# Transposes first, a first projection step of one channel block, and bursts of the modulation tied to chunks

## The chip, the cores and the metric

One core of a Trainium2 chip runs the whole kernel as one program. The metric is the device time of one execution in microseconds (us), from start to end, median of several runs. Engines are called PE (TensorE matmul), PEld (its weight loads), DVE (VectorE), ACT (ScalarE), POOL (GpSimd) and SP (SyncE, which here only issues transfers).

## The reference, cut to what matters

One decoder layer for 256 prompt tokens and 32 sample tokens (8 sequences of 4), 288 tokens in all, model width 2048. The part at issue is the beginning of the layer:

```python
mod = jax.nn.silu(c) @ w_ada + b_ada            # w_ada 2048 x 12288
sh1, sc1, gt1, sh2, sc2, gt2 = jnp.split(mod, 6, axis=-1)
u = ada_modulate(rms_norm(x, norm1_g), sh1, sc1)  # h * (1 + scale) + shift
proj = u @ w_in                                  # w_in 2048 x 9232, split into q k v z a b xpool ga gb
```

Then come a convolution, a gated delta rule, causal pooling, two projections merged by gates, `w_out`, and a feed-forward part; the change touches none of that.

## The kernel before, in words

All activations are kept with channels on the partitions and the 288 tokens along the free axis. The 2048 channels are 16 blocks of 128. A projection is computed in three matmuls for one product: weights and activations are each split into a high part (`wh`, a cast on ACT) and a low part (`wl`, a subtraction on DVE or POOL), and `gemm` adds high times high, high times low and low times high in PSUM. Weights come as chunks of two channel blocks by 512 columns through five `raw` buffers; a chunk gives 24 matmuls of 128x128 by 128x288 into four PSUM banks, which an `evac` function empties.

The modulation is computed by `ada`, a generator. Each of its steps loads rows of `w_ada` and adds their share into one PSUM bank; the last step copies the bank (`adasb`), transposes it and adds the bias into `mod`. The six 2048-wide parts need 16 loads of rows each. Because the projection of a channel block needs `mod` of that block alone, the kernel begins with few blocks: `STEPS` lists the blocks per stage, (0,2), (2,4), (4,8), (8,12), (12,16). In each stage nine panels of 512 columns (`FIRST`) are multiplied with the blocks of the stage and added to nine accumulators `acc` in SBUF. Beside the matmuls of one stage, `fill` runs the generator of the next stage's modulation: after each chunk `fill()` adds `every` to a counter and takes a step for each whole unit.

Ahead of the first stage the inputs are loaded: the three tiles `xt` of x, the constants with the identity `ident` (`cfix`), the conditioning vectors `cs8` and `cp1`, and the small vectors `ra` and `rb`. x is normed (square on ACT, a power on POOL, scaling on DVE), and `normed(q)` transposes four channel blocks on PE through PSUM tiles `px` that ACT copies into `xn`. Before the change only `normed(0)` stands ahead of the first stage and the other three stand in its loop body. In each stage DVE makes `gsc`, applies scale and shift to `xn`, ACT rounds the result to the high part `rq` and DVE takes the low part. `pab` is a narrow matmul on the modulated `xn`, and `pst` transposes of a convolution state.

The order on each engine is not the program's order: a scheduler sets it when the kernel is built, from the data dependencies and its own estimate of durations; an instruction under `tc.high_priority()` goes ahead of others that are ready. `in_turn` keeps the modulation's matmuls in their own order. At run time every engine works off its list strictly in order and waits at an instruction until its operands are there. Transfers are issued by SP in such a list too.

Of the kernel before, what the change touches and what calls it, by code (L numbers as in the profile page):

```python
# [9 lines left out]
F32 = mybir.dt.float32  # L10
# [5 lines left out]
P = 128  # L16
# [8 lines left out]
KB = 2  # L25
# [48 lines left out]
def tile_step(ctx: ExitStack, tc: tile.TileContext, at, t):  # L74
# [29 lines left out]
    def load_raw(srcs, pool=None, kbs=KB):  # L104
        n = KB * 512
        if pool is None:
            raw = wpool.tile([P, n], F32, tag="raw", name="raw", bufs=RAW)
        elif pool is qp:
            raw = fquad("raw").rearrange("p k n -> p (k n)")[:, 0:n]
# [7 lines left out]
    def load_split(srcs, eng=vec):  # L117

        raw = load_raw(srcs)
        wh = [wpool.tile([P, 512], F32R, tag="wh", name="wh", bufs=WH) for _ in range(KB)]  # L120
        wl = [wpool.tile([P, 512], F32R, tag="wl", name="wl", bufs=WH) for _ in range(KB)]
        for i in range(KB):
            act.copy(wh[i], raw[:, i, :])  # L123
            eng.tensor_tensor(wl[i], raw[:, i, :], wh[i].bitcast(F32), ALU.subtract)  # L124
        return wh, wl

    def gemm(srcs_of, xs, evac, kbs, eng=vec, late=False):


        ps = [psg.tile([P, 512], F32, tag="g", name=f"g{j}") for j in range(4)]  # L130
        kbs = list(kbs)
        for c in range(0, len(kbs), KB):
            wh, wl = load_split(srcs_of(kbs[c]), eng)
            for j in range(4):
                o = ps[j][:, 0:N]
                last = c + KB == len(kbs)
                terms = [(w, x, i) for i in range(KB) for w, x in ((wh, 0), (wh, 1), (wl, 0))]
                if late and c == 0:
                    terms.sort(key=lambda v: v[1])
                for n, (w, x, i) in enumerate(terms):  # L140
                    pe.matmul(o, w[i][:, j * P:(j + 1) * P], xs(kbs[c + i])[x], start=c + n == 0,  # L141
                              stop=last and n == 3 * KB - 1)
# [5 lines left out]
    def cols_of(w, c0):  # L148
        return lambda kb: [(w[kb * P:(kb + KB) * P, c0:c0 + 512], 0, 512)]
# [30 lines left out]
    def ada(*d0s, n=16, pool=None):  # L180

        m = n * len(d0s)
        w = m // 4 * P
# [3 lines left out]
        pair = 2 if m == 8 else 1  # L187
        for c in range(0, 16, step * pair):
            loads = []
            for k in range(c, c + step * pair, step):  # L190
                raws = []
                for x in range(per):
                    if per > 1:
                        d = (d0s if len(d0s) > 1 else (d0s[0], d0s[0] + 8))[x]
                        srcs = [(t["w_ada"][0, k * P:(k + 1) * P, d * P:(d + 8) * P], 0, 1024)]
                    else:
                        srcs = [(t["w_ada"][0, k * P:(k + step) * P, d0 * P:(d0 + n) * P], i * n * P, (i + 1) * n * P)
                                for i, d0 in enumerate(d0s)]
                    raws.append(load_raw(srcs, qp if pool and d0s[0] == M_SH1 and k >= 8 else pool, step))
                loads.append((k, raws))  # L200

            todo = [(k, raws, i, j) for k, raws in reversed(loads) for i in range(step) for j in (2, 3, 0, 1)]
            for y, (k, raws, i, j) in enumerate(todo):
                x, q = divmod(j, 4 // per)
# [7 lines left out]
        for i in range(0, w, P):  # L212
            pe.transpose(ps[:, i:i + P], sb[:, i:i + P], ident)
        pv = ps[:, 0:w].rearrange("p (b q m) -> p q b m", q=4, m=32)
        k = 4 // len(d0s)
# [14 lines left out]
    class Fill:  # L230

        gen, every, n = iter(()), 1.0, 0.0

        def __call__(self):
# [11 lines left out]
    STEPS = ((0, 2), (2, 4), (4, 8), (8, 12), (12, 16))  # L246
# [59 lines left out]
    with tc.tile_pool(name="st", bufs=1) as st:  # L306
        cs8 = st.tile([P, P], F32, name="cs8")
        cp1 = st.tile([16, P], F32, name="cp1")
        xt = []
        for i, (src, n) in enumerate(((t["x_prompt"][0, 0:P], P), (t["x_prompt"][0, P:2 * P], P),  # L310
                                      (t["x_sample"].rearrange("b s d -> (b s) d"), NS))):
            xi = st.tile([n, DM], F32, name=f"xt{i}")
            dma(out=xi, in_=src)
            xt.append(xi)
            if i == 0:
                dma(out=cfix, in_=t["consts"][:, c0:c1])
                dma(out=cs8, in_=t["c_sample"].rearrange("b (k c) -> (b k) c", c=P))
                dma(out=cp1, in_=t["c_prompt"].rearrange("b (k c) -> (b k) c", c=P))
# [9 lines left out]
        begin = first_ada(*STEPS[0], st)  # L328
        for _ in range(2):
            next(begin)  # L330
        ra = st.tile([P, P], F32, name="ra")
        rb = st.tile([105, P], F32, name="rb")
        dma(out=ra[0:96, :], in_=t["b_ada"][0].rearrange("(r c) -> r c", c=P))
        dma(out=ra[96:112, :], in_=t["norm1_g"][0].rearrange("(r c) -> r c", c=P))
        dma(out=ra[112:128, :], in_=t["norm2_g"][0].rearrange("(r c) -> r c", c=P))
        dma(out=rb[0:96, :], in_=t["conv_w"][0].rearrange("j (r c) -> (j r) c", c=P))
        dma(out=rb[96:104, :], in_=t["pool_scale"][0].rearrange("(r c) -> r c", c=P))
        dma(out=rb[104:105, :], in_=t["o_norm_g"])
# [7 lines left out]
        drain(begin)  # L346
# [24 lines left out]
        normed(0)  # L371
# [3 lines left out]
        for n, (k0, k1) in enumerate(STEPS):  # L375
# [751 lines left out]
```

## Time and profile before

| what | value |
|---|---|
| median of 3 runs | 1842.74 us (1838.03 to 1844.19) |
| the profiled execution's own time | 1836.14 us |
| its span | 1834.4 us |
| PE busy | 1785.7 us (97%) |
| DVE, ACT, POOL busy | 986.2, 746.4, 206.7 us |
| granted TensorE clock, mean | 0.991 of full speed |
| bytes moved | 371.23 MB, mean 202 GB/s |

The profile is one execution; times in its rows count from the start of the span. Busy time of PE is no measure of work done, since a matmul's end is modelled; the distance between repeated groups in the chain of waits is the better measure. The granted clock stands as a share of 2.4 GHz.

### The profile page before, as it was taken

How to read it: one execution, taken by the hardware profiler on the slowest of the kernel's cores; microseconds unless marked ns; L12 is line 12 of the kernel's file. 1: busy time of each engine (PE TensorE's matmuls, PEld its weight loads, DVE VectorE, ACT ScalarE, POOL GpSimd, SP SyncE). 2: the span in 40 equal slices, each digit the busy share in tenths (PEclk: the TensorE clock that was granted, in tenths of full speed). 3: DMA queues.
4: the chain of work that ended last, by engine and by line, in shares of the span. 5: the costliest groups of instructions: out<-in, count | busy, mean ns of one | idle time of the engine just before them, and what ended most of it. 6: DMA issues, size and time to landing. Idle time of an engine off the chain costs nothing.

```text
span 1834.4 us, 37797 instructions
## 1 busy us (share of the span) xinstructions
PE 1785.7 (97%) x14778; PEld 1657.4 (90%) x14778; DVE 986.2 (54%) x2126; ACT 746.4 (41%) x1522; POOL 206.7 (11%) x376
## 2 busy tenths in 40 slices
PE   5999999999999999999998999999999999999997
PEld 4889998878988787889988999999999999999997
DVE  2466579665645665565555444454444454444454
ACT  4533356433444232344443443443333444444333
POOL 1000025340102232211142000000000000000000
PEclk9999999999999999999999999999999999999999
DMA  9898766666676584876566766655555555555552
GB/s 305 289 322 276 227 204 199 211 213 201 213 244 219 170 253 162 264 255 199 175 217 202 218 198 195 213 181 166 165 168 163 170 163 163 164 169 163 161 160 98
DMA packets 227210, 371.23 MB, mean 202 GB/s; under 512 B 18335, under 2 KB 118168, under 8 KB 226608
## 3 DMA queue, kind: packets, MB, share of 16 engines
q1 hardware_dynamic: 223224, 357.02, 61.0%
q0 software_dynamic: 3808, 11.80, 2.1%
q8 instruction: 116, 1.90, 0.4%
q14 instruction: 62, 0.51, 0.1%
HBM read 361.16 MB, written 7.96 MB: 201 GB/s over the span
## 4 chain that ended last, share of the span: by engine, by line
PE 86%; DMA 6%; DVE 5%; ACT 1%; issue 1%; SPq 0%; POOL 0%; POOLq 0%; ACTq 0%; DVEq 0%
PE g L141 76%; PE ada L206 4%; DMA raw<-in_w_in_dram 3%; DMA raw<-in_w_ada_dram 2%; DVE cy L274 1%; DVE wl L124 1%; PE pss L746 1%; DVE rq L1028 1%; ACT wh L123 1%; PE pks L700 1%; PE py L872 0%; SPq L114 0%; PE py L631 0%; PE pp L636 0%; DMA pw<-in_pool_w_dram 0%
## 5 line engine op out<-in xcount | busy, mean ns | idle before, releaser
L141 PE MATMUL g<-rq,wh 128*128 128x288 f32 x7296 | 1493.2, 299 | 10.3 <-ACT wh L123 4.0
L141 PEld LDWEIGHTS g<-rq,wh 128*128 128x128 f32 x7296 | 1172.9, 188 | 64.4 <-issue 22.7
L141 PE MATMUL g<-rq,wl 128*128 128x288 f32 x3648 | 1075.2, 296 | 0.7 <-POOL wl L124 0.7
L124 DVE TENSOR_TENSOR wl<-raw,wh 128x512 fp32r<-128x512 f32 x910 | 598.8, 692 | 661.4 <-ACT wh L123 659.8
L123 ACT CAST wh<-raw 128x512 fp32r<-128x512 f32 x944 | 543.9, 618 | 878.5 <-PE g L141 630.3
L141 PEld LDWEIGHTS g<-rq,wl 128*128 128x128 f32 x3648 | 687.6, 189 | 7.4 <-issue 4.5
L206 PE MATMUL ada<-raw,cpad 128*32 128x512 f32 (+2 forms) x1152 | 106.6, 473 | 15.3 <-DMA raw<-in_w_ada_dram 14.9
L168 POOL TENSOR_TENSOR ro<-ro,cfix 128x1 f32<-128x1 f32 (+1 forms) x3 | 1.7, 557 | 844.1 <-DVE ro L1091 844.1
L423 DVE TENSOR_TENSOR acc<-acc,g 128x288 f32<-128x288 f32 x144 | 62.2, 449 | 22.7 <-PE g L141 22.4
L206 PEld LDWEIGHTS ada<-raw,cpad 128*32 128x32 f32 x1152 | 28.0, 113 | 39.3 <-issue 19.4
L124 POOL TENSOR_TENSOR wl<-raw,wh 128x512 fp32r<-128x512 f32 x34 | 46.6, 1393 | 45.7 <-ACT wh L123 45.4
L141 PE MATMUL g<-q,wh 128*128 128x288 f32 x256 | 51.0, 294 | 0.0
L274 DVE SCALAR_TENSOR_TENSOR cy<-xc,vb,cy 128x312 f32<-128x312 f32 x72 | 43.6, 623 | 5.3 <-ACT cy L272 4.7
L141 PEld LDWEIGHTS g<-q,wh 128*128 128x128 f32 x256 | 41.3, 189 | 0.0
L141 PE MATMUL g<-q,wl 128*128 128x288 f32 x128 | 37.9, 296 | 0.0
L935 DVE SCALAR_TENSOR_TENSOR x<-g,mod,x 128x256 f32<-128x256 f32 x48 | 23.0, 480 | 12.5 <-PE g L141 11.5
L1061 DVE TENSOR_TENSOR fgg<-fgg,g 128x288 f32<-128x288 f32 x44 | 20.0, 454 | 10.9 <-PE g L141 8.7
L141 PEld LDWEIGHTS g<-q,wl 128*128 128x128 f32 x128 | 24.0, 188 | 0.0
L749 DVE SCALAR_TENSOR_TENSOR sst<-sst,cds,pss 128x128 f32<-128x128 f32 x64 | 18.1, 343 | 7.9 <-PE pss L746 7.7
L1056 DVE SCALAR_TENSOR_TENSOR fgg<-fth,fgg 128x288 f32<-128x288 f32 x44 | 20.0, 455 | 3.9 <-ACT fgg L1055 1.3
L1054 ACT ACTIVATE fth<-g 128x288 f32<-128x288 f32 x44 | 18.1, 412 | 7.3 <-PE g L141 5.4
L644 POOL MEMSET T<- 32x64 f32 x8 | 1.1, 142 | 168.5 <-PE pab L432 151.0
(324 smaller groups left out, 948.4 us busy)
## 6 DMA issues: line engine op xcount, KB each, us to landing
raw<-in_w_gate_up_dram SPq DMA_DIRECT2D x352, 256.0 KB, 3.1
raw<-in_w_in_dram SPq DMA_DIRECT2D x144, 512.0 KB, 5.3
raw<-in_w_ada_dram SPq DMA_DIRECT2D x128, 512.0 KB, 4.4
raw<-in_w_down_dram SPq DMA_DIRECT2D x88, 512.0 KB, 3.8
raw<-in_w_ada_dram SPq DMA_DIRECT2D x128, 256.0 KB, 5.5
raw<-in_w_out_dram SPq DMA_DIRECT2D x32, 512.0 KB, 3.7
raw<-in_w_proj_b_dram SPq DMA_DIRECT2D x16, 512.0 KB, 4.6
raw<-in_w_proj_a_dram SPq DMA_DIRECT2D x16, 512.0 KB, 5.0
```

Source lines behind the costliest of these rows:

```text
L123: act.copy(wh[i], raw[:, i, :])
L124: eng.tensor_tensor(wl[i], raw[:, i, :], wh[i].bitcast(F32), ALU.subtract)
L141: pe.matmul(o, w[i][:, j * P:(j + 1) * P], xs(kbs[c + i])[x], start=c + n == 0, stop=last and n == 3 * KB - 1)
L206: in_turn(pe.matmul(ps[32 * j:32 * j + 32, 0:w], cpad[:, k + i, :], raws[x][:, i, q * w:(q + 1) * w], start=c == 0 and y < 4, stop=c + ste ...
L274: vec.scalar_tensor_tensor(y[:, 0:L], xc[:, m:m + L], vb[:, 24 * m + no:24 * m + no + 1], y[:, 0:L], ALU.mult, ALU.add)
L423: vec.tensor_tensor(a, a, ps, ALU.add)
L700: pe.matmul(pks[NS * i:NS * i + NS, x * P:(x + 1) * P], km[i // 2][:, i % 2, b, :], S[i][:, b, :], start=b == 0, stop=b == NB - 1)
L746: pe.matmul(pss, kt[r, 0, :], wx[b0 // 4][r].rearrange("p b v -> p (b v)"), start=True, stop=True)
L935: vec.scalar_tensor_tensor(x[:, j, 0:NP], ps[:, 0:NP], mod[:, gate + d, 0:1], x[:, j, 0:NP], ALU.mult, ALU.add)
L1028: vec.scalar_tensor_tensor(b[:, d, 0:NP], hp, mod[:, M_SH2 + k, 0:1], a[:, d, 0:NP].bitcast(F32), ALU.add, ALU.subtract)
L1056: vec.scalar_tensor_tensor(gg, th, 1.0, gg, ALU.add, ALU.mult)
L1061: vec.tensor_tensor(gg, gg, ps, ALU.mult)
```

## The change

`STEPS` begins with (0,1), (1,2), (2,4). A chunk of the two one-block stages is one block by 512 columns (`kn`), so it gives 12 matmuls. `ada` learns to make one block of two parts (m = 2): four steps of four row blocks, ended by one matmul with `halves` in place of the transpose. All four `normed(q)` stand ahead of the first stage. The small loads `ra` and `rb` go to POOL's queue and stand early, `cs8`, `cp1` and `cfix` stand before x, and each x tile is loaded in two halves. In the first three stages the steps of the next modulation are tied behind the last matmul of a given chunk (`tc.issue_after`), with a counter set by stage. The first stage's evictions alternate between DVE and ACT, and POOL makes the low parts of three panels in the first stage and of all nine in the second. The copy to `adasb` gets high priority, and the extra buffers of the first modulation are dropped.

```diff
-    STEPS = ((0, 2), (2, 4), (4, 8), (8, 12), (12, 16))
+    STEPS = ((0, 1), (1, 2), (2, 4), (4, 8), (8, 12), (12, 16))
@@ gemm
+        kn = min(KB, len(kbs))
+        for c in range(0, len(kbs), kn):
+            wh, wl = load_split(srcs_of(kbs[c]), eng, kn)
...
-            fill()
+            fill(mm)
@@ ada
-        w = m // 4 * P
+        w = max(m // 4, 1) * P
-        pair = 2 if m == 8 else 1
+        pair = 2 if m in (4, 8) and d0s[0] != M_SH1 else 1
+        step = min(step, 4)
...
-        act.copy(sb[:, 0:w], ps[:, 0:w])
...
+        with tc.high_priority():
+            act.copy(sb[:, 0:w], ps[:, 0:w])
+        if m == 2:
+            pe.matmul(ps[:, 0:64], sb[:, 0:P], halves, start=True, stop=True)
@@ Fill
+        def __call__(self, mm):
             self.n += self.every
             while self.n >= 1:
                 self.n -= 1
-                next(self.gen, None)
+                with tc.issue_after(mm.ins) if self.behind else nullcontext():
+                    next(self.gen, None)
@@ loads
+        dma(out=cs8, in_=t["c_sample"].rearrange("b (k c) -> (b k) c", c=P))
+        dma(out=cp1, in_=t["c_prompt"].rearrange("b (k c) -> (b k) c", c=P))
+        dma(out=cfix, in_=t["consts"][:, c0:c1])
+        dmg(out=ra[0:96, :], in_=t["b_ada"][0].rearrange("(r c) -> r c", c=P))
...
-            dma(out=xi, in_=src)
+            for h in (0, 1024):
+                dma(out=xi[:, h:h + 1024], in_=src[:, h:h + 1024])
@@ stages
-        normed(0)
+        for q in range(4):
+            normed(q)
...
-            if n == 0:
-                for q in range(1, 4):
-                    normed(q)
-            if n == 1:
+            if n == 2:
...
-            fill.every = 8 / (dn // KB * len(FIRST) - 5) if more else 0.4
+            fill.every, fill.n = ((1, -4), (0.5, 0.5), (1, 0), (0.6, 0), (0.6, 0))[n] if more else (0.4, 0)
+            fill.behind = n < 3
...
-                        act.copy(a, ps)
+                        if j % 2:
+                            vec.tensor_copy(a, ps)
+                        else:
+                            act.copy(a, ps)
...
-                gemm(cols_of(w_in, c0), parts(uh, ul), evac, range(k0, k1), gp if n + p == 0 or not more and p % 2 else vec)
+                gemm(cols_of(w_in, c0, min(dn, KB)), parts(uh, ul), evac, range(k0, k1),
+                     gp if (p % 3 == 0 if n == 0 else n == 1 or not more and p % 2) else vec)
```

PE's list of before, from the last transposes that stand between the first chunk and the second. `px` are transposes of x, `ada` steps of the modulation, `g_328` to `g_331` the four banks of the first chunk, `g_393` on those of the second.

```order
L141 MATMUL g_331<-rq,wh 128x288 x2
L141 MATMUL g_331<-rq,wl 128x288
L367 MATMUL px<-cfix,xt_97 128x128 x4
L206 MATMUL ada<-raw,cpad 32x128 x8
L367 MATMUL px<-cfix,xt_92 128x128 x4
L206 MATMUL ada<-raw,cpad 32x128 x8
L432 MATMUL pab<-xn_233,wab 32x288 x2
L367 MATMUL px<-cfix,xt_97 128x128 x4
```

PE's list of the changed kernel from the end of the first modulation (the matmul with `cth`, which holds `halves`) to the first chunk.

```order
L217 MATMUL ada<-cth,adasb 128x64
L376 MATMUL px<-cfix,xt_106 128x128 x4
L376 MATMUL px<-cfix,xt_103 128x128 x4
L444 MATMUL pab<-xn_193,wab 32x288
L376 MATMUL px<-cfix,xt_109 128x32 x4
L376 MATMUL px<-cfix,xt_106 128x128 x4
L376 MATMUL px<-cfix,xt_103 128x128 x4
L376 MATMUL px<-cfix,xt_109 128x32 x4
L376 MATMUL px<-cfix,xt_103 128x128 x4
L376 MATMUL px<-cfix,xt_109 128x32 x4
L140 MATMUL g_287<-rq,wh 128x288
```

The twelve groups of transposes now all stand ahead of the first projection matmul, and `pab` waits among them for the modulated first block.

ACT's list of the changed kernel over the same stretch: copies of transposes (`xn`), the cast of weight chunks (`wh`), the copy of the modulation (`adasb`) and the rounding of the first block (`rq`).

```order
L378 COPY xn_193<-px 128x4x128
L121 CAST wh<-raw 128x512 x2
L378 COPY xn_193<-px 128x4x128
L215 COPY adasb<-ada 128x128
L378 COPY xn_212<-px 128x4x128
L121 CAST wh<-raw 128x512
L378 COPY xn_193<-px 128x4x32
L121 CAST wh<-raw 128x512 x2
L378 COPY xn_212<-px 128x4x128
L378 COPY xn_231<-px 128x4x128
```

Two weight casts stand ahead of the copy of the modulation and three more ahead of the remaining copies of transposes.

PE's list of the changed kernel where the first stage (`g_549` to `g_552` are its last chunk) hands over to the second (`g_581`).

```order
L209 MATMUL ada<-raw,cpad 32x128 x8
L140 MATMUL g_549<-rq,wh 128x288 x2
...
L140 MATMUL g_552<-rq,wh 128x288 x2
L140 MATMUL g_552<-rq,wl 128x288
L217 MATMUL ada<-cth,adasb 128x64
L444 MATMUL pab<-xn_193,wab 32x288
L417 MATMUL pst<-cfix,scv 128x24 x12
L140 MATMUL g_581<-rq,wh 128x288
```

The modulation of the second stage ends behind the last chunk of the first, and nothing but `pab` and `pst` stands between it and the next stage; before, the same end (`L213`) stood four chunks ahead of the first stage's end.

## Rows read from the trace of the kernel before

**Rows 1.** The page: busy tenths of PE in 40 slices of the span.
```profile
PE   5999999999999999999998999999999999999997
```
**Rows 2.** Windows: stretch, length, busy of PE, PEld, DVE, ACT, POOL, clock, DMA share, GB/s.
```profile
20.00:25.00 5.00, 4.65 (x60) 3.02 (x64) 2.07 (x3) 0.59 (x1) 0.54 (x1) 1.00 1.07 362
25.00:30.00 5.00, 3.15 (x58) 2.04 (x59) 0.91 (x4) 2.06 (x5) 1.56 (x2) 1.00 1.07 383
...
35.00:40.00 5.00, 5.00 (x51) 4.47 (x53) 0.39 (x1) 0.80 (x2) 0.00 (x0) 0.73 1.06 381
40.00:45.00 5.00, 3.65 (x37) 2.63 (x30) 2.59 (x4) 4.98 (x13) 0.00 (x0) 0.95 0.93 322
45.00:50.00 5.00, 5.00 (x35) 4.84 (x38) 0.71 (x2) 2.53 (x8) 0.00 (x0) 0.70 1.06 379
```
**Rows 3.** Windows of the second and the third stage of before.
```profile
79.70:118.70 39.00, 39.00 (x356) 33.07 (x356) 28.73 (x64) 12.41 (x23) 0.35 (x2) 1.00 0.91 312
118.70:188.70 70.00, 69.58 (x602) 62.36 (x598) 40.42 (x83) 22.07 (x39) 0.00 (x0) 1.00 0.87 288
```
**Rows 4.** The chain of waits: start, length, what.
```profile
0.75 4.98 DMA xt<-in_x_prompt_dram
6.16 8.04 DMA raw<-in_w_ada_dram
...
84.21 0.85 PE pst L410 x12
...
128.40 6.59 PE g L141 x48
135.00 1.00 PE ada L206 x16
```
**Rows 5.** Timeline from the last modulation step to the first projection matmul.
```profile
25.92 0.65 PE L206 MATMUL ada<-raw,cpad 128*32 128x128 f32 x16 [0.38 <-DMA raw<-in_w_ada_dram]
...
27.75 0.62 ACT L123 CAST wh<-raw 128x512 fp32r<-128x512 f32 x1 [2.15 <-DMA raw<-in_w_in_dram]
28.27 0.26 ACT L211 COPY adasb<-ada 128x128 f32<-128x128 f32 x1
...
29.85 1.56 DVE L388 TENSOR_SCALAR xn<-xn,gsc,mod 128x256 f32<-128x256 f32 x2
...
31.89 0.67 ACT L395 CAST rq<-xn 128x576 fp32r<-128x576 f32 x1 [2.68 <-DVE xn L392]
...
32.62 0.79 PE L141 MATMUL g<-rq,wh 128*128 128x288 f32 x4 [1.50 <-ACT rq L395]
```
**Rows 6.** Groups by line and form, 0 to 240 us: busy us, mean ns.
```profile
L124 DVE TENSOR_TENSOR wl<-raw,wh 128x512 fp32r<-128x512 f32 x100 | 65.0, 687 | 66.5 <-ACT wh L123 66.5
...
L423 DVE TENSOR_TENSOR acc<-acc,g 128x288 f32<-128x288 f32 x97 | 42.3, 451 | 19.6 <-PE g L141 19.4
...
L369 ACT COPY xn<-px 128x512 f32<-128x512 f32 x8 | 4.6, 588 | 14.2 <-PE px L367 14.2
...
L395 ACT CAST rq<-xn 128x1152 fp32r<-128x1152 f32 x3 | 3.5, 1155 | 2.4 <-DVE xn L392 2.4
...
L124 POOL TENSOR_TENSOR wl<-raw,wh 128x512 fp32r<-128x512 f32 x2 | 2.5, 1271 | 7.0 <-ACT wh L123 7.0
```
**Rows 7.** The scaling of xn on DVE, 0 to 240 us: ns min/median/max.
```profile
L388 DVE TENSOR_SCALAR xn<-xn,gsc,mod x16: 401/408/1237, 29.9 to 229.7; 128x256 f32<-128x256 f32 x16
```
**Rows 8.** Timeline at the end of the second stage of before.
```profile
112.51 1.38 DVE L388 TENSOR_SCALAR xn<-xn,gsc,mod 128x256 f32<-128x256 f32 x4
...
118.42 0.69 PE L432 MATMUL pab<-xn,wab 128*32 128x288 f32 x8
```
**Rows 9.** Windows of 20 us with a shorter and a longer wait of PE.
```profile
280.00:300.00 20.00, 18.74 (x142) 16.46 (x139) 19.00 (x36) 13.07 (x34) 12.75 (x25) 1.00 0.68 215
...
380.00:400.00 20.00, 17.86 (x109) 14.70 (x110) 11.50 (x38) 7.30 (x23) 7.69 (x11) 0.83 0.72 222
```
**Rows 10.** Window of the load of the narrow weights (wab).
```profile
33.00:34.00 1.00, 1.00 (x10) 0.80 (x9) 0.36 (x1) 1.00 (x4) 0.00 (x0) 1.00 1.06 141
```

More of the change, by code (lines that the diff above doesn't have):

```diff
@@ L115, in load_raw, with load_split @@
         return raw
[L117 to L124, printed above, removed]
+    def load_split(srcs, eng=vec, kn=KB):
+        raw = load_raw(srcs, kbs=kn)
+        wh = [wpool.tile([P, 512], F32R, tag="wh", name="wh", bufs=WH) for _ in range(kn)]
+        wl = [wpool.tile([P, 512], F32R, tag="wl", name="wl", bufs=WH) for _ in range(kn)]
+        for i in range(kn):
+            act.copy(wh[i], raw[:, i, 0:512])
+            eng.tensor_tensor(wl[i], raw[:, i, 0:512], wh[i].bitcast(F32), ALU.subtract)
         return wh, wl
@@ L131, in gemm @@
         kbs = list(kbs)
-        for c in range(0, len(kbs), KB):
-            wh, wl = load_split(srcs_of(kbs[c]), eng)
+        kn = min(KB, len(kbs))
+        for c in range(0, len(kbs), kn):
+            wh, wl = load_split(srcs_of(kbs[c]), eng, kn)
             for j in range(4):
                 o = ps[j][:, 0:N]
-                last = c + KB == len(kbs)
-                terms = [(w, x, i) for i in range(KB) for w, x in ((wh, 0), (wh, 1), (wl, 0))]
+                last = c + kn == len(kbs)
+                terms = [(w, x, i) for i in range(kn) for w, x in ((wh, 0), (wh, 1), (wl, 0))]
                 if late and c == 0:
@@ L140, in gemm @@
                 for n, (w, x, i) in enumerate(terms):
-                    pe.matmul(o, w[i][:, j * P:(j + 1) * P], xs(kbs[c + i])[x], start=c + n == 0,
-                              stop=last and n == 3 * KB - 1)
+                    mm = pe.matmul(o, w[i][:, j * P:(j + 1) * P], xs(kbs[c + i])[x], start=c + n == 0,
+                                   stop=last and n == 3 * kn - 1)
                 if last:
@@ L198, in ada @@
                                 for i, d0 in enumerate(d0s)]
-                    raws.append(load_raw(srcs, qp if pool and d0s[0] == M_SH1 and k >= 8 else pool, step))
+                    raws.append(load_raw(srcs, pool, step))
                 loads.append((k, raws))
             todo = [(k, raws, i, j) for k, raws in reversed(loads) for i in range(step) for j in (2, 3, 0, 1)]
+            if m == 2:
+                todo = [(k, raws, i, 2 * (i % 2) + h) for k, raws, i, j in todo if j == 0 for h in (1, 0)]
             for y, (k, raws, i, j) in enumerate(todo):
-                x, q = divmod(j, 4 // per)
+                x, q = divmod(j % m, 4 // per)
                 with tc.high_priority() if y else nullcontext():
@@ L210, in ada @@
         sb = wpool.tile([P, 512], F32, tag="adasb", name="adasb", bufs=1)
-        act.copy(sb[:, 0:w], ps[:, 0:w])
[L212 to L215, printed above, removed]
+        with tc.high_priority():
+            act.copy(sb[:, 0:w], ps[:, 0:w])
+        if m == 2:
+            pe.matmul(ps[:, 0:64], sb[:, 0:P], halves, start=True, stop=True)
+            pv = ps[:, 0:64].rearrange("p (b q m) -> p q b m", q=2, m=32)
+            k = 1
+        else:
+            for i in range(0, w, P):
+                pe.transpose(ps[:, i:i + P], sb[:, i:i + P], ident)
+            pv = ps[:, 0:w].rearrange("p (b q m) -> p q b m", q=4, m=32)
+            k = 4 // len(d0s)
         for i, d0 in enumerate(d0s):
@@ L230, in tile_step @@
     class Fill:
-        gen, every, n = iter(()), 1.0, 0.0
-        def __call__(self):
+        gen, every, n, behind = iter(()), 1.0, 0.0, False
+        def __call__(self, mm):
             self.n += self.every
@@ L308, in tile_step @@
         cp1 = st.tile([16, P], F32, name="cp1")
+        dma(out=cs8, in_=t["c_sample"].rearrange("b (k c) -> (b k) c", c=P))
+        dma(out=cp1, in_=t["c_prompt"].rearrange("b (k c) -> (b k) c", c=P))
+        dma(out=cfix, in_=t["consts"][:, c0:c1])
+        ra = st.tile([P, P], F32, name="ra")
+        rb = st.tile([105, P], F32, name="rb")
+        dmg(out=ra[0:96, :], in_=t["b_ada"][0].rearrange("(r c) -> r c", c=P))
+        dmg(out=ra[96:112, :], in_=t["norm1_g"][0].rearrange("(r c) -> r c", c=P))
+        dmg(out=ra[112:128, :], in_=t["norm2_g"][0].rearrange("(r c) -> r c", c=P))
+        dmg(out=rb[0:96, :], in_=t["conv_w"][0].rearrange("j (r c) -> (j r) c", c=P))
+        dmg(out=rb[96:104, :], in_=t["pool_scale"][0].rearrange("(r c) -> r c", c=P))
+        dmg(out=rb[104:105, :], in_=t["o_norm_g"])
         xt = []
@@ L327, in tile_step @@
                                  chf.rearrange("p (m k) -> p m k", k=16), ALU.add, ALU.mult)
[L328 to L338, printed above, removed]
+        halves = cth[:, 0:64]
+        gp.tensor_tensor(halves, ident[:, 0:64], ident[:, 64:P], ALU.add)
         pv = aux("pv")
```

13 lines of the change are left out of this document (4 added, 9 removed).

## Prediction

> **What bounds the kernel now.** I read the page first, then windows, then the chain of waits, then timelines. On the page PE is busy in every slice but the first [rows 1]: whatever this change gains, it gains in the first 190 us, where the stages of the first projection stand. There the chain begins with transfers: x, then the first modulation's weights (8.04 us in one piece) [rows 4]; in the timeline the last step of that modulation runs at 25.92 us, and the first projection matmul follows at 32.62 [rows 5]. From then on PE is full, with two blemishes: ACT is full from 40 to 45 us while PE waits for transposes, and the clock is at 0.73 and 0.70 in two windows, that is at the lower of its two levels for part of them, after PE had idled [rows 2]. The second stage of before takes 39.0 us with PE busy all the time, the third 70.0 us with 0.42 us idle [rows 3]. In these stages a projection matmul costs 6.59/48 = 0.137 us and 16 modulation records 1.00 us [rows 4].
>
> So the change can move three things: when the first projection matmul starts, what is lost inside the first two channel blocks, and what is lost between stages. Later work is the same in kind and count.
>
> **The start.** The first modulation shrinks from two blocks to one: 16 transfers of 256 KB become 8, 4.2 MB become 2.1 MB, but the rows become half as long (512 bytes in place of 1024), 4096 of them as before. No row of before shows rows of 512 bytes in number, so I bound: at the rate by bytes, 362 to 383 GB/s where transfers queue [rows 2], 2.1/0.37 = 5.7 us; if each row costs as much as one of 1024 bytes, 4.2/0.37 = 11.3 us. I take 6.5 us, near the first end, as bytes have set the rate in every busy window. The Trainium skill (DMA: Bandwidth & Descriptors, section "Why small descriptors are slow") speaks against the short rows: each packet carries a fixed overhead of about 3 beats beside one beat for 32 bytes, so 19 beats for 512 bytes against 35 for 1024. By that rule alone, an estimate, the load takes 5.7 x 38/35 = 6.2 us; no row of before shows it.
>
> Step by step: the first transfer of x is issued at 0.75 and 1.05 MB of it has landed at 5.73 [rows 4]; at 0.37 MB per us that is 2.8 us of data behind 2.15 us of latency, so data flows from 2.9 us. x and the small inputs, 2.5 MB, are in at 9.7, the modulation at 16.2, the first two weight chunks (0.52 MB) at 17.6. ACT's list has two weight casts and one copy ahead of the copy `adasb`: 0.62 + 0.59 + 0.26 us [rows 5, 6] make it 19.1, so the modulation ends behind the weights, as it did at 27.75 and 28.27 [rows 5]. The next three chunks wait for `wab`, whose transfer of tiny rows pulled the rate to 141 GB/s at a full DMA share [rows 10]; I price it at 1.5 us, and chunks three to five are cast by 17.6 + 1.5 + 3 x 0.65 + 0.65 = 21.7. Behind them ACT has five copies of 0.59 [rows 6] and two of tiles a quarter as wide, about 0.29 each by their share and a fixed part, about 1.5 us of waits between PE and ACT over two PSUM tiles, and the rounding of one block (half of 0.67, rows 5): 5.4 us. First projection matmul at 27.3, against 32.62. The loads moved off SP's list to POOL's queue end before 12 us and nothing waits for them; POOL is free there.
>
> **First stage, one block.** 9 panels x 12 matmuls = 108 x 0.137 = 14.8 us, and the second modulation, 64 records at 0.65/16 [rows 5], 2.6 us. Six of the twelve groups of transposes stood in this stretch in before; they are gone from it. ACT has per panel one cast and two evictions, DVE a subtraction and two, less than PE's 1.65 us. One spell at the lower level of the clock when the work sets in, as in before: 0.73 and 0.70 over 5 us are 1.35 and 1.5 us lost, with edges in the neighbouring window (0.95) [rows 2]: 1.7 us. End at 46.4.
>
> **Handovers.** The new cost. A stage's modulation now ends in or behind the last chunks of the stage before, so the chain from there to the rounded blocks lies open. First to second: matmul with `halves` 0.2, bias and scale vector 0.8, scaling of one block 0.35 to 0.8, samples 0.45, then `pab` and the 12 `pst` transposes, 0.85 [rows 4], which also need their own late load: 3.1 us, 2.0 of them idle. Second to third: DVE's list has the last evictions, 2 scalings (0.35 each, by 4 in 1.38) [rows 8], samples, a weight subtraction, then the rounding 0.67 [rows 5]: 3.2 us, 2.85 idle. Third to fourth: four scalings 1.38, two subtractions 1.3, the last eviction and small ones 1.5, rounding 1.15 [rows 6, 8], together 5.4 us, of which two bursts and `pab` cover 2.8; idle 2.6, against about 0.6 in before. Queued behind the waiting PE are only projection matmuls, and nobody but DVE and ACT evictions waits for these.
>
> In before the scaling took 0.78 us a block while POOL made low parts, up to 1.24 against a median of 0.41 [rows 5, 7]. POOL now makes 12 in the first two stages, each 1.27 us [rows 6]; I count one collision, in the first handover. The Trainium skill (SBUF — State Buffer, section "Who interferes with whom") says that DVE and GpSimd lock a common port pair for a whole instruction; the trace agrees, 1.24 us against 0.41. By that rule each of the first two handovers could wait one such instruction, 1.3 us more each.
>
> **Second stage, one block.** 14.8 us, its bursts 128 records at 0.65/16 = 5.2, the other `pst` 0.85. DVE has 36 additions of 0.45 and some six subtractions of 0.65 [rows 6], 20.1 us against PE's 20.8, so I add 1.0 for banks that come free late: 21.8 us.
>
> **Third stage** is before's second (blocks 2 and 3, the same bursts): 39.0 less 1.7 of `pst` and 0.3 of `pab`, 37.0 us. **From the fourth on** the stages are before's third to fifth.
>
> **The sum.** 27.3 + 17.4 + 1.7 = 46.4; + 3.1 + 21.8 = 71.3; + 3.2 + 37.0 = 111.5. Before reaches this point at 118.4 [rows 8]. 6.9 us ahead; less 2.0 for the longer third handover, 4.9. Handovers also cost clock: a window with 1.26 us of idle PE kept 1.00, one with 2.14 us shows 0.83 [rows 9]. I count one spell of 1.7 us in expectation (three handovers, about half each is 2.5; the third is broken up by bursts). 3.2 us faster: 1836.14 - 3.2 = 1832.9 against the profiled execution. The median is 6.6 us above that execution, and I carry the difference over: 1842.74 - 3.2 = **1839.5 us**.
>
> **Rivals.** *Clearly faster:* casts do not hold the copies up (first matmul at 24.5, 2.8 earlier), no clock spell in a handover (1.7), DVE keeps up (1.0): 8.7 us, 1834.0. For it: ACT is busy only 0.59 of 20 to 25 us in before [rows 2]. Against: its list puts the casts first, and they wait for transfers.
>
> *Slower:* the bursts tied to chunks wait for their transfers. In the third stage each chunk with its burst needs 1.57 MB in 24 x 0.137 + 1.00 = 4.3 us, 366 GB/s; two bursts are loaded ahead, six are not. Each us lost per period counts six times, so the gain is gone when a period takes 4.3 + 3.2/6 = 4.8 us, at 325 GB/s. At 288, the mean of the next stage in before [rows 3], a period takes 5.45 and the loss is 6 x 1.15 = 6.9, so 3.7 us slower than before: 1846.4; from 273 GB/s down it is slower by more than a measurement's reach. For it: the tie takes away the scheduler's freedom. Against: where transfers queue, windows show 362 to 383 GB/s [rows 2], and before drew the same bytes through the same buffers with PE full [rows 3].
>
> *The short rows cost as long ones:* 4.8 us later start, 1844.3, no change that can be told.
>
> *It does not do what it says:* the lists show that transposes, blocks and bursts stand where the change puts them, so this is small.
>
> **Chances.** Forecast as worked out 0.42, clearly faster 0.28, slower 0.14, short rows 0.12, something else 0.04. About 0.3% (5.5 us) is what a measurement can tell from no change. Faster by more needs below 1837.2: nearly all of the second case and a tenth of the first, 0.32. Slower by more needs above 1848.3: the third case mostly, and what the reordering behind 190 us may bring, 0.16. The same: 0.52. Range 1830 to 1848.5: the low end is all of the clearly faster case and handovers as cheap as before's; the high end takes in the short rows, two more clock spells and a late `pst` load.
>
> **What would show it.** Right: first projection matmul near 27 us, idle gaps of 2 to 3 us at three handovers, near 46, 71 and 112 us, third stage near 37 us, fourth beginning 3 to 5 us earlier than 118.7. Wrong: a start after 31 us; waits of PE for `w_ada` transfers in the third stage; a difference that arises behind 190 us, where I expect none.

## The result, and the profile after

| | kernel before | changed kernel |
|---|---|---|
| median of 10 runs each | 1841.78 us | 1851.75 us |
| lowest to highest | 1834.8 to 1844.19 | 1846.55 to 1857.74 |
| the profiled execution's own time, its span | 1836.14, 1834.4 us | 1854.41, 1852.6 us |
| granted TensorE clock, mean | 0.991 | 0.985 |

The ratio is 1.0065, 95% interval 1.0045 to 1.0085: slower by 0.65%, where I forecast 1839.5 us and gave slower 0.16. The profiled execution of the changed kernel is 2.7 us above its median and that of before 5.6 below its own, so of the 18.3 us between the two profiles 10.0 are in the medians. The page's slices answer to [rows 1]: busy tenths of PE, then the granted clock.

```profile
PE   6899999989999999999999999999999999999997
...
PEclk8999999989999999999999999999999999999998
```

The weaker second slice (46 to 93 us) is new, and so is the one around 390 us, with a lower clock. The windows of the changed kernel answer to [rows 2]:

```profile
20.00:25.00 5.00, 3.68 (x37) 2.36 (x35) 3.52 (x8) 3.50 (x8) 2.24 (x2) 1.00 0.87 254
25.00:30.00 5.00, 3.22 (x18) 2.04 (x18) 1.04 (x2) 3.19 (x7) 0.30 (x1) 0.74 0.88 254
30.00:35.00 5.00, 4.28 (x19) 3.82 (x20) 0.73 (x2) 1.87 (x5) 0.00 (x0) 0.50 0.92 281
35.00:40.00 5.00, 5.00 (x30) 5.00 (x30) 3.36 (x8) 3.44 (x9) 1.44 (x1) 0.73 0.73 224
...
50.00:55.00 5.00, 2.53 (x31) 2.19 (x30) 3.42 (x9) 2.14 (x6) 2.55 (x2) 0.97 0.97 321
55.00:60.00 5.00, 4.59 (x22) 3.58 (x23) 0.71 (x3) 0.84 (x2) 0.35 (x2) 0.50 0.74 232
```

Two things stand out: a first projection that starts at half the clock, 1.2 in place of 2.4 GHz (0.50 from 30 to 35 us; before works so at its start too, for less time [rows 2]), and a hole at 52 us, where PE is busy 2.53 of 5 us and works at half the clock afterwards (0.50). The timeline of the changed kernel shows this first handover, from block 0 to block 1:

```profile
52.20 0.33 PE L217 MATMUL ada<-cth,adasb 128*128 128x64 f32 x2
...
53.00 1.26 POOL L122 TENSOR_TENSOR wl<-raw,wh 128x512 fp32r<-128x512 f32 x1 [1.07 <-ACT wh L121]
53.04 1.25 DVE L387 SCALAR_TENSOR_TENSOR gsc<-mod,va 128x9 f32<-128x9 f32 x1
54.32 0.41 DVE L398 TENSOR_SCALAR xn<-xn,gsc,mod 128x256 f32<-128x256 f32 x1
...
55.11 1.17 PE L444 MATMUL pab<-xn,wab 128*32 128x288 f32 x2 [2.58 <-DVE xn L402]
...
56.58 1.44 PE L417 MATMUL pst<-cfix,scv 24*128 24x24 f32 x12 [0.30 <-DMA scv<-in_state_conv_dram]
57.95 0.74 PEld L140 LDWEIGHTS g<-rq,wh 128*128 128x128 f32 x3
```

The end of the second modulation (the matmul with `halves`, L217) stands behind the last chunk of the first stage. From there PE has nothing to do until DVE has made `gsc` and `xn`: 2.58 us. `gsc`, 0.17 us at 80 us, takes 1.25 beside POOL's subtraction. Then `pab` and `pst` run at half the clock, and the first matmul of block 1 stands at 57.95, 5.6 us after the last of block 0. The waits of PE in the changed kernel from 50 to 130 us (total, times, longest) show this wait at all three handovers: 2.58, 2.67 and 0.31 us. The third handover waits 1.0 us for modulation weights besides.

```profile
PE pab L444 <- DVE xn L402: 5.6, 3, 2.7
PE ada L209 <- DMA raw<-in_w_ada_dram: 1.0, 1, 1.0
```

In time, by the end of the last eviction of each stage:

| end of blocks | before | changed | difference |
|---|---|---|---|
| 0 and 1 | 79.96 | 81.28 | +1.3 |
| 2 and 3 | 118.98 | 123.25 | +4.3 |
| 4 to 7 | 188.96 | 196.19 | +7.2 |
| 8 to 11 | 256.45 | 266.26 | +9.8 |
| 12 to 15 | 329.69 | 342.25 | +12.6 |

Where an expectation below names such an end, it counts 0.24 us less. The remaining 5.7 us of the two profiles lie behind 342 us, where the work is the same; there the changed kernel's execution spends 38.6 us at half the clock, before 27.2.

Where the 12.6 us are can be counted from two windows, before first and the changed kernel second (in the fences, row 1 is 32 to 196 us, row 2 is 196 to 330):

```profile
32.00:196.00 164.00, 161.61 (x1410) 141.72 (x1411) 89.25 (x182) 65.72 (x133) 0.35 (x2) 0.98 0.89 296
196.00:330.00 134.00, 131.62 (x1010) 119.64 (x1010) 99.23 (x220) 70.26 (x156) 37.97 (x74) 1.00 0.65 204
```

```profile
32.00:196.00 164.00, 155.65 (x1401) 136.16 (x1405) 102.65 (x223) 54.17 (x103) 13.38 (x12) 0.96 0.85 284
196.00:330.00 134.00, 129.13 (x998) 116.19 (x991) 94.28 (x212) 65.77 (x150) 36.20 (x74) 0.99 0.67 213
```

Idle time of PE in the first stretch: 2.4 us before, 8.4 after. The clock's share that is missing: 0.02 x 164 = 3.3 before, 0.04 x 164 = 6.6 after. In the second stretch idle time is 2.4 and 4.9, and the clock costs 1.3 more. Sum: 6.0 + 3.3 + 2.5 + 1.3 = 13.1, against 12.6 by the ends of the stages. The two agree partly by chance: up to blocks 4 to 7 the terms give 9.3 against 7.2, since seven of the twelve groups of transposes (28 matmuls) stand behind the first projection matmul in before and ahead of it in the changed kernel, less two bursts that before has ahead of it, an estimate of some 2 us; behind that they give 3.8 against 5.3. So waits and half-clock work make up the loss, to within about 2 us on either side of 196 us.

The clock's share is not all behind handovers. These windows split it, two of the changed kernel and then two of before:

```profile
32.00:52.60 20.60, 20.53 (x178) 18.88 (x178) 10.17 (x22) 12.51 (x31) 7.91 (x6) 0.86 0.81 242
52.60:61.50 8.90, 6.09 (x34) 4.79 (x38) 4.43 (x12) 1.62 (x4) 1.61 (x3) 0.62 0.72 237
```

```profile
32.00:79.70 47.70, 45.73 (x404) 39.66 (x405) 16.16 (x30) 29.25 (x70) 0.00 (x0) 0.93 0.90 298
79.70:83.70 4.00, 4.00 (x39) 3.25 (x39) 2.21 (x6) 1.04 (x3) 0.00 (x0) 1.00 0.72 192
```

In the changed kernel 0.14 x 20.6 = 2.9 us lie in the start of the projection and 0.38 x 8.9 = 3.4 behind the first handover; the other two handovers have 1.00. Before loses 0.07 x 47.7 = 3.3 in its start and nothing in its handover at 80 us, where PE is busy all 4.0 us. Up to 196 us the extra clock is that of the first handover alone.

### The profile page after: what moved, and what is told of

Read it like the earlier page. It is cut to its first block, busy times and chain, and to the rows that moved or that the text cites. A ratio compares the mean times of both kernels' runs of the same rounds, so it can differ in the third digit from the quotient of the medians.

```text
span 1852.6 us, 37896 instructions
## 1 busy us (share of the span) xinstructions
PE 1792.3 (97%) x14781; PEld 1662.6 (90%) x14781; DVE 1004.7 (54%) x2176; ACT 742.1 (40%) x1506; POOL 220.8 (12%) x393
## 3 DMA queue, kind: packets, MB, share of 16 engines
q1 hardware_dynamic: 227494, 356.90, 60.5%
## 4 chain that ended last, share of the span: by engine, by line
PE 91%; DMA 4%; DVE 2%; ACT 1%; issue 1%; SPq 1%; POOL 0%; POOLq 0%; ACTq 0%; DVEq 0%
PE g L140 79%; PE ada L209 5%; DMA raw<-in_w_ada_dram 2%; PE pss L758 1%; DMA raw<-in_w_in_dram 1%; DVE rq L1040 1%; PE pks L712 0%; DMA xt<-in_x_prompt_dram 0%; PE py L884 0%; SPq L112 0%; PE py L643 0%; DMA raw<-in_w_gate_up_dram 0%; DVE hp L1038 0%; PE pp L648 0%; DVE wl L122 0%
## 5 line engine op out<-in xcount | busy, mean ns | idle before, releaser
L434 DVE TENSOR_TENSOR acc<-acc,g 128x288 f32<-128x288 f32 x180 | 77.7, 450 | 31.9 <-PE g L140 31.7
L122 POOL TENSOR_TENSOR wl<-raw,wh 128x512 fp32r<-128x512 f32 x44 | 59.7, 1375 | 61.8 <-ACT wh L121 47.3
L947 DVE SCALAR_TENSOR_TENSOR x<-g,mod,x 128x256 f32<-128x256 f32 x48 | 23.0, 479 | 12.5 <-PE g L140 11.5
```

The lines of the kernel that those rows point to most:

```text
L122: eng.tensor_tensor(wl[i], raw[:, i, 0:512], wh[i].bitcast(F32), ALU.subtract)
L947: vec.scalar_tensor_tensor(x[:, j, 0:NP], ps[:, 0:NP], mod[:, gate + d, 0:1], x[:, j, 0:NP], ALU.mult, ALU.add)
```

## The experiments

My theory after reading the two traces was that the tie of the bursts to chunks lets each modulation end in the last chunk of its stage, so that three handovers lie open and drop the clock (A; the windows above show the drop at the first alone). Rivals: the transposes ahead hold the start up (B); the one-block steps by themselves cost (C); the new loads do (D); it is not the tie, but the counters `fill.n` and `fill.every`, which set the bursts late (E). The ratio is to the kernel before on the same chip. Idle is PE's from 32 to 196 us and the clock that of the same window, as above; the last column is the end of blocks 12 to 15 in us (in before 329.69).

| kernel | ratio, 95% interval | idle | clock | end |
|---|---|---|---|---|
| the change | 1.0065 [1.0045, 1.0085] | 8.4 | 0.96 | 342.25 |
| e2 transposes back in the loop | 1.0064 [1.004, 1.0088] | 11.5 | 0.97 | 341.86 |
| e8 unread matmuls in the handovers | 1.0041 [1.0022, 1.0061] | (2.2) | 0.98 | 337.03 |
| e5 tied, early counters | 1.0038 [1.0021, 1.0054] | 8.1 | 0.99 | 334.54 |
| e9 third stage untied | 1.0018 [1.0001, 1.0034] | 5.0 | 0.98 | 330.82 |
| e10 first two stages untied | 1.0011 [0.9997, 1.0025] | 3.5 | 0.98 | 332.67 |
| e6 untied, counters of the change | 1.0009 [0.9989, 1.003] | 2.1 | 1.00 | 327.93 |
| e7 two blocks first, untied | 1.0008 [0.9988, 1.0028] | 3.4 | 0.98 | 330.94 |
| e3 untied, early counters | 0.9998 [0.998, 1.0016] | 2.2 | 0.98 | 329.22 |
| e1 two blocks first | 0.9985 [0.9973, 0.9998] | 5.0 | 0.98 | 332.85 |
| e11 the same again | 1.0008 [0.9992, 1.0023] | 5.3 | 0.96 | 332.85 |
| e4 the loads alone | 0.9983 [0.9963, 1.0004] | 0.8 | 0.98 | 327.28 |
| e12 the same again | 0.9995 [0.9976, 1.0014] | 2.4 | 0.97 | 331.13 |

The unread matmuls of e8 count as busy, hence the brackets. One profile tells the end to within some 4 us (e4 and e12 are one kernel); in kernels that start with two blocks some of the idle time is a later start. The clock of one window is no sure sign either: e11 has 0.96 as the change has, and no loss.

**e1 and e11: a first stage of two blocks, bursts tied in the first two stages.** With the one-block second stage go its nine low parts on POOL, and the counters are early ones; the rest of the change is kept.

```diff
-    STEPS = ((0, 1), (1, 2), (2, 4), (4, 8), (8, 12), (12, 16))
+    STEPS = ((0, 2), (2, 4), (4, 8), (8, 12), (12, 16))
...
-            fill.every, fill.n = ((1, -4), (0.5, 0.5), (1, 0), (0.6, 0), (0.6, 0))[n] if more else (0.4, 0)
-            fill.behind = n < 3
+            fill.every, fill.n = ((1, 0), (1, 0), (0.6, 0), (0.6, 0))[n] if more else (0.4, 0)
+            fill.behind = n < 2
...
-                     gp if (p % 3 == 0 if n == 0 else n == 1 or not more and p % 2) else vec)
+                     gp if (p % 3 == 0 if n == 0 else not more and p % 2) else vec)
```

> The changed kernel with the old first step of two blocks, all else of the change kept (transposes ahead, new loads, tied bursts in the first two stages). Theory A (open handovers: each stage's modulation ends so late that the chain to the next stage's blocks lies open, 2.6 us of idle PE each, with clock spells): one handover of three is gone, about 4 us faster than the changed kernel, near 1848. Theory B (the transposes ahead of the first matmul cost the gain of the start): no gain, the first projection matmul later than 32.4 us, near 1852. Theory C (the one-block steps as such, with a chunk of 12 matmuls and an eviction per 12): near before, 1842 to 1844.

> The changed kernel with a first stage of two blocks, bursts tied in the first two stages, once more on another day and chip: it was 0.9985 [0.9973, 0.9998]. If it is really faster than the kernel before, the ratio is again below 1 and both intervals together exclude 1; if the first was chance, near 1.000 to 1.002, as the same kernel with free bursts was.

Measured 1839.98 us, and again 1841.5 (both on one chip, though the second expectation says another): the loss is gone, but together they are no gain over before. That is more than A expected (1848) and nearer to C, so the one-block steps are needed for the loss; whether they cost by themselves e3 tells. So the tie, with these counters, costs nothing where the first stage has two blocks; its modulation ends at 60.5 us there, well ahead of the end of the stage at 75.16. Neither the transposes ahead (B) nor the loads (D) cost, as both are in this kernel.

**e2: `normed(1)` to `normed(3)` back in the loop of the first stage.**

```diff
-        for q in range(4):
-            normed(q)
+        normed(0)
...
+            if n == 0:
+                for q in range(1, 4):
+                    normed(q)
```

> The changed kernel with three of the four groups of transposes back in the first stage. Theory B: first projection matmul at about 27 us in place of 32.4, blocks 0 and 1 done 4 to 6 us earlier, near 1847. Theory A: the transposes run later at the full clock, a gain of 2 us at most, and the three handovers are unchanged: near 1850.

Measured 1855.07, ratio 1.0064. B falls. Its timeline shows why the start does not gain; the first two rows are the rounding and the first projection matmul:

```profile
26.04 0.43 ACT L404 CAST rq<-xn 128x288 fp32r<-128x288 f32 x1
...
27.11 1.33 PE L140 MATMUL g<-rq,wh 128*128 128x288 f32 x4
...
31.02 2.82 PE L376 MATMUL px<-cfix,xt 128*128 128x128 f32 x16
...
34.64 0.30 PEld L140 LDWEIGHTS g<-rq,wh 128*128 128x128 f32 x2
```

The first projection matmul stands at 27.11, 5.3 us earlier than in the changed kernel, and then the transposes stand between the chunks: the first panel's eviction ends at 36.13 us, against 36.14. For the start the transposes cost the same in either place.

**e3: untied, and counters that do the modulations early.**

```diff
-            fill.every, fill.n = ((1, -4), (0.5, 0.5), (1, 0), (0.6, 0), (0.6, 0))[n] if more else (0.4, 0)
-            fill.behind = n < 3
+            fill.every, fill.n = ((1, 0), (1, 0), (2, 0), (0.6, 0), (0.6, 0))[n] if more else (0.4, 0)
+            fill.behind = False
```

> The changed kernel with the bursts not tied and due earlier in their stage (one step per chunk in the one-block stages, two per chunk in the third), as the old rate had it. Theory A: idle PE at the handovers goes from 2.6, 2.7 and about 2 us to under 1 each and two clock spells go: 6 to 9 us faster than the changed kernel, 1843 to 1846. Theory B: the start stays at 32 us and the gain is 2 us at most. A rival to A (bursts that come earlier wait for their transfers): idle PE before modulation steps rises by what the handovers give, near 1851.

Measured 1842.28, ratio 0.9998. The loss is gone with one-block steps and transposes ahead in place: C falls as far as it means a cost that must come with the steps. One-block steps and the tie cost together, and neither does alone (e3, e1). The timeline of e3 where the first stage ends has no hole, and adds of the second stage (L434) follow the last copy of the first (L430) at once:

```profile
56.69 0.46 DVE L430 COPY acc<-g 128x288 f32<-128x288 f32 x1 [1.53 <-PE g L140]
...
57.09 2.06 DVE L434 TENSOR_TENSOR acc<-acc,g 128x288 f32<-128x288 f32 x5
```

**e4 and e12: the kernel before with the loads of the change alone** (`cs8`, `cp1`, `cfix` ahead of x, x in halves, `ra` and `rb` on POOL's queue).

> The kernel before with the change's loads alone (small inputs first, x in halves, vectors on the POOL queue). If the loads cost (the POOL queue's packets or the order delay x and the first modulation): 2 to 4 us slower than before, 1844 to 1846. If they help: first projection matmul 2 to 3 us earlier than 32.6, 1839. Theories A and B: no loss from it, 1840 to 1842.

> The kernel before with the changed kernel's loads alone (order of the small loads, x in halves, two loads on POOL's queue), once more: it was 0.9983 [0.9963, 1.0004]. If these loads gain what the end of the first projection showed (327.0 us against 329.45 in the kernel before, 2.4 us), the ratio is 0.9987 again and both runs together lie below 1. If it was chance, 1.000 to 1.001.

Measured 1839.99 and 1841.93: no loss, and no gain that two runs bear out. D falls.

**e5: tied, with e3's counters.** The diff is e3's pair of lines on `fill.every` and `fill.n`, with `fill.behind = n < 3` kept.

> The changed kernel with its bursts still tied behind chunks, but due earlier (one step per chunk in the one-block stages, two in the third). If lateness is the cause: the handovers of the second and third stage close, 5 to 9 us faster than the changed kernel, 1843 to 1847. If the tie itself is the cause (PE waits in order for the burst's transfer): no gain, idle PE ahead of modulation steps of 5 us or more in sum, 1850 or later.

Measured 1846.79, ratio 1.0038: in between. The open handover is nearly gone from the waits of PE, 33 to 132 us, but another wait stands ahead of it:

```profile
PE ada L209 <- DMA raw<-in_w_ada_dram: 3.1, 3, 1.4
PE g L140 <- ACT acc L432: 1.1, 1, 1.1
...
PE pab L444 <- DVE xn L402: 0.3, 1, 0.3
```

Tied to early chunks, the bursts wait for their weights instead. Against e3, where the tie is the only difference, it is 0.40% slower, clear of both intervals: the tie costs without the late counters too. That lateness is a part of the tie's cost rests on less, 0.27% against an uncertainty of about 0.26, and on the handovers' wait (0.3 us against 5.6).

**e6: untied, with the counters of the change.**

```diff
-            fill.behind = n < 3
+            fill.behind = False
```

> The changed kernel with the tie alone taken away, its counters kept; the order of PE then has the modulation's end well before the end of the first two stages. If the tie is the cause: as good as the kernel with free and earlier bursts, 1842 to 1844. If the counters (which set how late a burst is due) are the cause: no gain, 1850 to 1853.

Measured 1842.91, ratio 1.0009, with the tie as the only difference: 0.56 of the 0.65% come back. Its view of L217 says how (ns min/median/max, first and last start); the changed kernel's is the second fence:

```profile
L217 PE MATMUL ada<-cth,adasb x4: 217/274/323, 22.4 to 38.2; 128*128 128x64 f32 x4
```

```profile
L217 PE MATMUL ada<-cth,adasb x4: 218/275/323, 22.0 to 52.3; 128*128 128x64 f32 x4
```

Untied, the second modulation ends at 38.2 us, 15 us ahead of the end of the first stage; tied, at 52.3, behind its last chunk. The counters are the same: without the tie the scheduler puts a burst where its weights are there. So E falls as a cause by itself: late counters without the tie cost nothing that can be told. The window of e6 to 196 us closes the account:

```profile
32.00:196.00 164.00, 161.95 (x1476) 141.97 (x1477) 106.59 (x233) 57.95 (x110) 13.18 (x12) 1.00 0.90 303
```

Idle time is 2.1 against 8.4 us and the clock 1.00 against 0.96: 6.3 + 6.6 = 12.9 us, and blocks 4 to 7 end 12.3 us earlier than in the changed kernel (183.89). Of the 6.6, 2.9 are the changed kernel's start, as the windows above show; in e6's execution the half-clock work of the start lies ahead of 32 us.

**e7: e1 with untied bursts at before's rate** (`fill.every = 8 / (dn // KB * len(FIRST) - 5)`, `fill.behind = False`).

> The old steps (two blocks first) with the new loads, all transposes ahead, and bursts free at the old rate: what is left of the change is its start. If the open handovers are the whole loss, the start's gain shows: blocks 0 and 1 done at about 75 us as in the kernel with two blocks and ties, no open handover behind, 1835 to 1838, faster than before by 4 to 7 us. If the start gives nothing in the end: 1840 to 1842.

Measured 1841.99, ratio 1.0008: with two blocks first the tie makes no difference that can be told (e1 and e11).

**e8: the change, with six matmuls of 128x256 whose results nobody reads, at the end of each of the first three stages:** in the first behind the matmul with `halves` (`fill.tail`), in the others behind the last projection matmul.

```diff
-            pe.matmul(ps[:, 0:64], sb[:, 0:P], halves, start=True, stop=True)
+            fill.tail = pe.matmul(ps[:, 0:64], sb[:, 0:P], halves, start=True, stop=True)
...
+            if n < 3:
+                warm = aux("warm", 2)
+                for _ in range(6):
+                    with tc.issue_after(fill.tail.ins if n == 0 else mm.ins):
+                        pe.matmul(warm[:, 0:256], ident, cpad.rearrange("p k m -> p (k m)")[:, 0:256], start=True, stop=True)
```

> The changed kernel with six matmuls of 128x128 by 128x256 behind the end of each of the first three stages, whose results nobody reads: PE is busy while the chain of the handover runs. If the spells at the lower clock are a part of the loss: the spell that begins at 54.7 us goes, blocks 0 and 1 are done 2 to 3 us earlier than 81.0, about 3 us faster, 1848 to 1850. If the chain alone counts: no change or up to 2 us slower, 1851 to 1854.

Measured 1847.17, ratio 1.0041: 0.24 of the 0.65% come back, which is not clear of the two intervals (some 0.28 together), and the handovers stay as long. The half-clock stretch behind the first one is shorter, 3.4 us (from 55.95) against 6.8 (from 54.74), but not gone, as `pst` there waits 1.4 us for its own load (0.3 in the changed kernel). That this is the work of the unread matmuls is not shown: e9, which has none, has 3.4 us there too (from 55.56). And e8 ends block 0 1.8 us ahead of the changed kernel, though the engines' lists up to there are the same in the two kernels, and block 1 only 0.9 ahead. So e8 does not tell what keeping PE busy is worth; what the clock costs is read from the windows of the changed kernel, 3.4 us behind the first handover.

**e9 and e10: untied in the third stage only, and in the first two only** (`fill.behind = n < 2`, and `n == 2`).

> The bursts are tied to chunks in the first two stages only; in the third they stand where the scheduler puts them. Theory (the two short handovers with their idle 2.6 us and the half-clock stretches behind them carry most of the cost of the tie): only the third stage (34.7 us from its first eviction to its last in the changed kernel, 32.9 without any tie) and the third handover (12.4 us against 10.7) come back, 3.6 us; blocks 4 to 7 end near 192.4 us (195.95 in the changed kernel, 183.65 without any tie), median near 1848.5, ratio 1.004. Rival (the third stage's tied bursts are what costs): the median comes back to 1843, ratio within 1.001.

> The reverse: tied in the third stage only. Theory: the first two handovers close, 9 us earlier at the end of blocks 4 to 7 (near 187 us), median near 1845, ratio 1.002; PE shows no wait over 1.3 us between 30 and 90 us. Rival (third stage): nothing comes back but what the idle time itself was worth, median 1849 to 1851.

Measured 1844.66 (1.0018) and 1841.72 (1.0011). The gains do not add: 0.47 and 0.54%, and 0.56 with both. By the end of blocks 4 to 7, in one execution each, they do: 7.3 and 5.7 us, and 12.3 with both (e6). What does not add lies behind, where no burst is tied. Both times came back further than I expected, e10's though its blocks 4 to 7 end at 190.45, not near 187. Of e9's 7.3 us, 4.4 lie between the end of block 1 and the first evicted panel of blocks 4 to 7, near the 3.6 expected; the rest lies ahead of the stage that was changed, a start 1.0 us earlier and a shorter half-clock stretch at 55 us. Its first handover keeps its wait (2.6). Besides, both kernels have no longer wait than 0.8 and 1.0 us in place of one that the changed kernel has later:

```profile
PE ada L209 <- DMA raw<-in_w_ada_dram: 3.3, 1, 3.3
```

This one of the changed kernel, at 272.85 us, has a half-clock stretch from 276.61 behind it, and the stage of blocks 12 to 15 takes 70.0 us from its first evicted panel, against 65.8 in e9. e6 and e1 have it too, with 2.4 and 2.0 us, so it is not the tie's alone; why the third stage's order moves it was not tried.

## Why the prediction was wrong

**What held.** The handovers are where I put them, two of them with the idle time forecast: 2.58 and 2.67 us, where I wrote 2.0 and 2.85. The second stage took 22.2 us (forecast 21.8), the handover to the third 3.37 (3.2). The rival of tied bursts that wait for transfers in the third stage did not come true there. The chain of waits of the changed kernel has a period of 4.39 us, where I said 4.3, and no wait in it:

```profile
87.25 1.00 PE ada L209 x16
88.25 3.40 PE g L140 x24
91.64 1.00 PE ada L209 x16
92.64 3.39 PE g L140 x24
```

**The step that failed: the start.** "First projection matmul at 27.3" was the whole gain; it stood at 32.40, against 32.62 before. The term behind it is the rate of the first transfers. I took 0.37 MB per us from 2.9 us on, and 6.5 us for the modulation's 2.1 MB; the windows of the changed kernel show less:

```profile
0.00:10.00 10.00, 1.11 (x3) 0.54 (x3) 0.56 (x2) 3.76 (x5) 4.94 (x17) 1.00 0.72 241
10.00:15.00 5.00, 0.32 (x8) 0.35 (x12) 1.48 (x3) 2.86 (x3) 1.10 (x2) 1.00 1.14 269
15.00:18.00 3.00, 2.69 (x37) 1.79 (x29) 2.35 (x3) 1.15 (x2) 0.54 (x1) 1.00 1.11 334
18.00:21.00 3.00, 3.00 (x38) 1.77 (x36) 0.89 (x5) 1.70 (x3) 0.55 (x1) 1.00 0.97 217
```

Up to 10 us they carry 2.41 MB, where I had 2.63: 0.6 us late. From 10 to 18 us, where nearly all of the modulation's short rows run, they carry 5 x 0.269 + 3 x 0.334 = 2.35 MB, so its load took close to 8 us, 1.5 more than my 6.5. From 18 to 21 us, with weight chunks and the short rows of `wab`, the rate is 217 GB/s, which is 1.2 us late again. Only from 15 to 18 us is it 334 GB/s, at which 2.1 MB take 6.3 us. By the Trainium skill (DMA: Bandwidth & Descriptors, "Why small descriptors are slow") it was 6.2, an estimate; this row comes near it, the load as a whole does not.

So the fifth chunk is cast by 25.87, not 21.7 (+4.2, of which these rows show 3.3; what made the other 0.9 is open), as the timeline shows. The copies of the transposes then alternate with PE at half the clock and end the start at 32.4 (+0.9; the terms add to 27.1, and the prediction carries 27.3):

```profile
25.25 0.62 ACT L121 CAST wh<-raw 128x512 fp32r<-128x512 f32 x1 [1.29 <-DMA raw<-in_w_in_dram]
...
31.20 0.58 ACT L378 COPY xn<-px 128x512 f32<-128x512 f32 x1 [1.21 <-PE px L376]
31.68 0.43 ACT L405 CAST rq<-xn 128x288 fp32r<-128x288 f32 x1
...
32.40 1.57 PE L140 MATMUL g<-rq,wh 128*128 128x288 f32 x5
```

e2 shows what a start at 27.1 would have been worth by itself: nothing, since the transposes then come between the chunks. I counted them ahead of the start and also took them out of the first stage, but allowed nothing for PE at half the clock between their copies.

**The first handover** took 5.6 us in place of 3.1, +2.5. I named its three parts (a collision with POOL, `pab` and `pst`, the clock), but gave the collision a part of its price, and `pab` and `pst` full clock: 1.17 and 1.44 us, together 2.6, where I had 0.85. Some of this is chance: in e9, whose engines have the same lists up to there, `pab` ran at full clock and the handover took 4.6 us.

**The third stage** took 39.0 us, not 37.0: 9 x 3.39 + 8 x 1.00 is 38.5 by the chain. I had subtracted `pst` and `pab` from a stage of before that took 39.0, without counting its bursts; +2.0. The first stage was 0.9 longer, the others 0.55. Together 5.1 + 0.9 + 2.5 + 0.55 + 2.0 = 11.05: the third stage's last matmul ended at 122.6, where I had 111.5. The third handover, with the stage behind it, cost 3.0 us against before, not 2.0. I had 1.7 for the clock in the sum, which the measured terms contain: at 196 us I was off by 11.05 + 1.0 - 1.7 = 10.4 us, from 3.2 ahead to 7.2 behind.

**Behind 196 us** I expected no difference. The trace has 5.3 us there up to 342 (the wait at 272.85, its clock, and 1 us in the order of the bursts: e3 takes 141.7 us from the end of blocks 4 to 7 to the end, before 140.7).

**The weights of the cases.** I judged a gain in the start against a cost in the handovers, and took both as certain by their sizes. The cost needed only the order to be kept, which the lists showed; the gain needed transfers, ACT and the clock all to go well. The "slower" rival had the right sign and the wrong mechanism: not transfers that come late, but modulations that end late.

**What stays open:** how much clock a handover costs by itself (3.4 and 6.8 us at half the clock behind the same handover in e9 and the changed kernel), what e8's matmuls are worth, and what makes the stages behind 196 us differ.

No version here beats the kernel before by more than can be told: e1 and e4 lay 0.15 to 0.17% below it once, and their second runs did not bear it out.

## What to carry to other kernels

Work that is tied to a place (here a modulation to the chunks of the stage ahead of it) must end early enough for the whole chain behind it, not just before it is needed: ask what the last piece's consumers do, engine by engine, and count that chain as idle time of the bound engine. Splitting a first step in two buys an earlier start only if the transfers ahead of it really run at full rate, and it buys one more handover for certain, which cost nothing that can be told only where the order was left free (e3, e6). Price a wait with the half-clock work that may stand behind it: here the first handover waited 2.6 us and lost 3.4 more to the clock, the second waited 2.7 and lost nothing to it.

## What the runs showed of the hardware

- Two waits of the same length had different ends. After the 2.58 us at 52.52 the granted clock is 0.50 from 55 to 60 us; after the 2.67 us at 80.18 it stays at 1.00 in the stretch from 81 to 88.3. Ahead of both, PE had been working at a clock of 1.00 (45 to 50 and 61.5 to 81 us). What followed differed: `pab` and 12 small transposes, with another 0.30 us of waiting, behind the first, `pab` and at once projection matmuls behind the second. The window of the second:

```profile
81.00:88.30 7.30, 5.43 (x45) 3.92 (x46) 4.76 (x12) 1.81 (x3) 0.00 (x0) 1.00 0.53 180
```

- An instruction of DVE on 9 columns took 1.25 us in place of 0.17, and one on 32 columns (L402) 1.22 in place of 0.19, each beside a subtraction on POOL of 1.26 us. The Trainium skill (SBUF — State Buffer, "Who interferes with whom") says that the two lock a common port pair for a whole instruction. The trace agrees: both DVE instructions ended within 0.05 us of the subtraction on POOL, however small they were.
